# Attention by pairs of heads: probabilities copied out once as plain float32, value products with 64 output rows into the two halves of a bank, no fold by DMA

## The chip, the cores and the metric

The kernel runs on one core of one Trainium2 chip. The metric is the device time of one execution in microseconds: 4202.87 us in the median of three runs (4188.57 to 4209.19). Five engines work beside each other: PE (TensorE, matrix products and transposes into the eight banks of PSUM), DVE (VectorE), ACT (ScalarE), POOL (GpSimd), and SP, which issues the DMAs. Each runs its own instructions in order and waits at semaphores for the others.

## The reference

Two layers of a transformer-like trunk over 1152 tokens: 128 prompt tokens and 1024 sample tokens. A layer projects its input into three groups of heads, mixes each, projects back, and adds a feed-forward part. The three mixers are a gated recurrence (HGRN, 4 heads), attention with compressed keys and values (MLA, 6 heads, keys of 96 columns, values of 64) and attention with shared keys (GQA, 6 heads of 64 columns on 2 key heads). What the change touches is the attention, for both kinds:

```
s = jnp.einsum('bqhgd,bkhd->bhgqk', qi, k, preferred_element_type=F32) * scale
p = jax.nn.softmax(s, axis=-1)
return jnp.einsum('bhgqk,bkhe->bqhge', p.astype(v.dtype), v)
```

Sample queries (8 tiles of 128) read 128 cached keys and the 1024 sample keys, that is 9 key tiles; prompt queries (one tile) read the 128 prompt keys alone. All is float32.

## The kernel before

A layer has four phases: B (in-projection and HGRN), C (attention), D (output projection, first norm) and E (feed-forward, second norm). Large products are made in three terms of split operands: `split` rounds an operand to float32r (`hi`) and keeps the exact rest (`lo`), and `mm3` (L110 to L112) adds hi*hi, hi*lo and lo*hi. A float32r product is one pass on PE, a plain float32 product is recorded as two.

Phase C (`phase_c`) runs GQA, then MLA, through the same loop, `attention`. A *group* is one head and two query tiles; there are 24 groups in GQA and 24 in MLA in each layer. For a group, `probs` makes the scores of each query tile in three banks of 384 keys (L799; 2 products a bank in GQA, 3 in MLA), their maxima on DVE (L800, L803), and the exponentials with their sums on ACT (L805). The nine key tiles of the probabilities are then turned, two at a time, in five *turns* (`turn`): four transposes on PE into a bank `c` (L820), and the split of the bank into `hi` and `lo` (tiles `pt`). In four turns ACT rounds (L103) and DVE subtracts (L104). In the first turn of a group (`POOL_TURNS`) ACT copies the bank to `px` (L824), DVE rounds (L825) and Pool subtracts (L826). The value product (L869) has as its weights the 64 high and the 64 low columns of the values beside each other, so its 128 output rows are the products with the high and with the low part; it runs over the 256 columns of `hi` and again over those of `lo`. After nine key tiles DVE multiplies the bank `d` by the reciprocals of the sums (L873; `inv_sums` has brought them along the free axis through DRAM, `rind` and `rb`), a DMA moves one half of the rows across to the other partitions (L770), and Pool adds the halves (L771, `out_rows`) into the mixed activations `mx(j)`.

The scores run ahead of the turns by `LEAD` pieces (a piece is one bank of scores), the turns ahead of the value products by `AHEAD`; `NPT` and `NP` are the buffers of turned tiles and of probabilities. With every second turn one piece of other work (`self.aside`) is taken in: during GQA the backward states of HGRN (`hgrn_back`, L739 on PE), the turning of the second key head's queries and keys (`gqa_turn`), the turning of MLA's compressed operands (`mla_turn`) and the prompt's attention (`prompt_attention`: scores L884, transposes L899, values L906); during MLA each head's keys (`prep_k`), queries (`prep_q`, tiles `qg` of 512 columns and `qp` of the prompt), values (`prep_v`) and its prompt's attention. `prep_k` makes the keys of both heads of a pair, as the two halves of its output rows, and uses one half; it does so for each head.

The order of the instructions on each engine isn't that of the text: a scheduler places them within the limits of buffers and dependences. The PSUM banks of phase C are rings: scores in `b` (3) and `a` (2), turns in `c` (2), value sums in `d` (1).

Of the kernel before, what the change touches and what calls it, by code (L numbers as in the profile page):

```python
# [7 lines left out]
F32 = mybir.dt.float32  # L8
# [8 lines left out]
P = 128  # L17
D = 1024
# [20 lines left out]
W_OUT_ORDER = (0, 1, 7, 2, 5, 6, 3, 4)  # L39


def mixed(a, b, n):
    """n pieces of a, then one of b, and so on."""
# [10 lines left out]
class Build:  # L54
# [24 lines left out]
    def banks(self, **tags):  # L79
        """PSUM banks of the phase that starts: tag -> the rings its tiles come from, in turn."""  # L80
# [17 lines left out]
    def split(self, hi, lo, src, eng=None, vec=False):  # L98
        """hi = src rounded to float32r, lo = the exact rest."""
# [6 lines left out]
    def mm3(self, out, terms):  # L106
        """out = sum of a.T @ b over terms of split operands (ah, al, bh, bl)."""
# [6 lines left out]
    def rsq(self, out, ss, scale, cols):  # L114
        """out = (ss * scale + EPS) ** -0.5"""
# [37 lines left out]
    def floors(self):  # L153
        """the second layer's lower bounds of the gates, and one minus them."""
# [19 lines left out]
    def ada(self, l, part):  # L174
        """part: 0 sh1, 1 sc1, 2 g1, 3 sh2, 4 sc2, 5 g2. A generator of eight pieces of work."""
# [32 lines left out]
    def ada0(self):  # L208
        """the first layer's sh1 and sc1."""
# [44 lines left out]
    def coefs(self, l, which, ln):  # L254
        """(scale, shift) [P, 8, 2] of the modulation; with ln = (layer, norm) that norm's gain and bias are in them."""
# [12 lines left out]
    def make_hT(self, coefs, ci, xt, dst, phase):  # L268
        """dst [P, 8, 2, 384]: (x * scale + shift).T of the token tiles 3 ci .. 3 ci + 2."""
# [22 lines left out]
    def stats(self, u):  # L292
        """one over the deviation, and the mean, of the rows."""
# [10 lines left out]
    def norm(self, u):  # L304
        """layer norm without gain and bias, in place."""
# [17 lines left out]
    # ================= in-projection and HGRN =================  # L323
# [1118 lines left out]
```

## Time and profile before

| | |
|---|---|
| median of three runs | 4202.87 us (4188.57 to 4209.19) |
| span of the profiled execution | 4234.5 us |
| PE busy in it | 3772.9 us (89%) |
| DVE busy | 2251.7 us (53%) |
| ACT busy | 1587.9 us (38%) |
| POOL busy | 1330.6 us (31%) |

The busy time of an engine is the union of its instructions' records. PE's products overlap each other, and their ends are modelled, so a busy PE isn't a PE at its peak; how soon one product starts after the one before says more. Shares over the whole span mix phases with different limits, so the phases are read apart.

### The profile page before, as it was taken

The page shows a single profiled execution, that of the slowest core. Times are in us where ns is not written, and L with a number is a line of the kernel's source. Part 1 is how long each engine was busy: PE and PEld are TensorE (multiplying, and loading weights), DVE is VectorE, ACT ScalarE, POOL GpSimd, SP SyncE. Part 2 cuts the span into 40 slices and gives each one's busy share as a digit, 9 for nine tenths or more (in the row PEclk, how much of TensorE's full clock was granted, in tenths as well). Part 3 has the DMA queues.
Part 4 walks back from the last instruction along what each step waited for, and adds up shares of the span by engine and source line. Part 5 has one row for each costly group of instructions (what it writes and reads, how often), then busy time and mean ns, then how long its engine had stood idle before and what let it go on. Part 6 is the DMA issues. An engine that isn't in the chain of part 4 may idle for free. (4 is left out here: it accounts for less than half of the span.)

```text
span 4234.5 us, 58490 instructions
## 1 busy us (share of the span) xinstructions
PE 3772.9 (89%) x21820; PEld 3429.4 (81%) x21820; DVE 2251.7 (53%) x4256; ACT 1587.9 (37%) x3576; POOL 1330.6 (31%) x1558
## 2 busy tenths in 40 slices
PE   8999867777799999999999987777777999999997
PEld 7987756677679899999989877666766799999996
DVE  5688355555566434443366883654544743333336
ACT  5543455555433122122144335655553421111111
POOL 1277552232126000000432876513222650000043
PEclk9988988988899999999999988888888999999999
DMA  6322533211224222222331114221112221111121
GB/s 213 111 74 63 142 43 41 25 15 14 42 69 137 73 75 80 65 75 72 104 123 57 52 45 106 48 37 21 14 20 59 74 93 50 40 45 45 40 90 70
DMA packets 235207, 282.13 MB, mean 67 GB/s; under 512 B 98057, under 2 KB 163721, under 8 KB 234538
## 3 DMA queue, kind: packets, MB, share of 16 engines
q1 hardware_dynamic: 234922, 278.38, 24.9%
q8 instruction: 172, 2.82, 0.3%
q14 instruction: 113, 0.93, 0.1%
HBM read 231.05 MB, written 38.87 MB: 64 GB/s over the span
## 5 line engine op out<-in xcount | busy, mean ns | idle before, releaser
L111 PE MATMUL b<-h,w 128*128 128x384 f32 x1848 | 623.5, 337 | 5.2 <-DVE h L104 5.2
L112 PE MATMUL b<-h,w 128*128 128x384 f32 x1848 | 623.2, 337 | 2.1 <-DVE w L104 2.1
L110 PE MATMUL b<-h,w 128*128 128x384 f32 x1848 | 624.1, 338 | 0.4 <-ACT w L103 0.4
L104 DVE TENSOR_TENSOR w<-raw,w 128x1024 fp32r<-128x1024 f32 (+2 forms) x268 | 342.1, 1285 | 397.6 <-ACT w L103 337.6
L103 ACT CAST w<-raw 128x1024 fp32r<-128x1024 f32 (+2 forms) x272 | 281.4, 1039 | 675.7 <-PE b L111 236.2
L1258 POOL TENSOR_TENSOR acc<-acc,lg 128x512 f32<-128x512 f32 x36 | 50.8, 1428 | 1283.7 <-DVE acc L1244 1278.9
L111 PEld LDWEIGHTS b<-h,w 128*128 128x128 f32 x1848 | 348.5, 189 | 11.5 <-DVE h L104 6.4
L110 PEld LDWEIGHTS b<-h,w 128*128 128x128 f32 x1848 | 348.3, 189 | 9.9 <-issue 2.6
L112 PEld LDWEIGHTS b<-h,w 128*128 128x128 f32 x1848 | 348.5, 189 | 6.0 <-DVE w L104 2.4
L820 PE MATMUL c<-ident,p 128*128 128x128 f32 x1728 | 308.2, 302 | 35.6 <-ACT px L824 16.2
L104 DVE TENSOR_TENSOR pt<-c,pt 128x512 fp32r<-128x512 f32 (+2 forms) x404 | 240.4, 603 | 155.4 <-ACT pt L103 150.8
L110 PE MATMUL a<-w,h 128*128 128x256 f32 (+1 forms) x960 | 285.2, 297 | 2.9 <-ACT st L406 1.1
L103 ACT CAST pt<-c 128x512 fp32r<-128x512 f32 (+2 forms) x404 | 206.8, 526 | 211.3 <-PE c L820 180.2
L820 PEld LDWEIGHTS c<-ident,p 128*128 128x128 f32 x1728 | 231.5, 156 | 63.3 <-ACT px L824 19.8
L111 PE MATMUL a<-w,h 128*128 128x256 f32 (+1 forms) x960 | 282.6, 294 | 0.0
L112 PE MATMUL a<-w,h 128*128 128x256 f32 (+1 forms) x960 | 281.9, 294 | 0.0
L771 POOL TENSOR_TENSOR m<-u 64x256 f32<-64x256 f32 (+1 forms) x120 | 80.3, 669 | 621.0 <-DMA u<-u 555.1
L869 PE MATMUL d<-pt,V 128*128 128x256 f32 x864 | 202.0, 342 | 72.1 <-POOL pt L826 44.3
L800 DVE TENSOR_REDUCE m<-b 128x1 f32<-128x384 f32 x356 | 195.0, 553 | 117.2 <-PE b L799 114.9
L869 PE MATMUL d<-pt,v 128*128 128x256 f32 x864 | 188.7, 330 | 62.5 <-DVE u L873 21.6
L805 ACT ACTIVATE p<-b,nm 128x384 f32<-128x384 f32 x356 | 205.2, 585 | 98.5 <-DVE nm L803 77.5
L869 PEld LDWEIGHTS d<-pt,V 128*128 128x128 f32 x864 | 147.2, 221 | 87.1 <-POOL pt L826 49.9
(395 smaller groups left out, 9451.7 us busy)
## 6 DMA issues: line engine op xcount, KB each, us to landing
raw<-in_w_ffn_in_dram SPq DMA_DIRECT2D x88, 512.0 KB, 3.5
raw<-in_w_ada_dram SPq DMA_DIRECT2D x80, 512.0 KB, 3.8
raw<-in_w_ffn_out_dram SPq DMA_DIRECT2D x44, 512.0 KB, 4.7
raw<-in_w_in_a_dram SPq DMA_DIRECT2D x32, 512.0 KB, 3.9
rb<-rind SPq DMA_DIRECT2D x96, 128.0 KB, 5.1
xs<-acc SPq DMA_DIRECT2D x36, 256.0 KB, 4.1
u<-xs SPq DMA_DIRECT2D x36, 256.0 KB, 3.1
w<-in_w_ada_dram SPq DMA_DIRECT2D x16, 512.0 KB, 6.7
```

What stands on the lines that cost most here:

```text
L103: self.nc.scalar.copy(hi, src)
L104: (eng or self.nc.vector).tensor_tensor(lo, src, hi.bitcast(F32), op=ALU.subtract)
L110: self.nc.tensor.matmul(out, ah, bh, start=i == 0, stop=False)
L111: self.nc.tensor.matmul(out, ah, bl, start=False, stop=False)
L112: self.nc.tensor.matmul(out, al, bh, start=False, stop=i == n - 1)
L771: nc.gpsimd.tensor_tensor(self.mx(hd // 2)[r:r + 64, cols], On[r:r + 64], sw[r:r + 64], op=ALU.add)
L800: nc.vector.reduce_max(mx[:, c:c + 1], ps, axis=AX.X)
L805: nc.scalar.activation(pt[:, c * 384:(c + 1) * 384], tiles[c], AF.Exp, bias=nm, accum_out=sm[:, i, c:c + 1])
L820: nc.tensor.transpose(pt[:, (2 * a + i) * P:(2 * a + i + 1) * P], g["p"][i][:, kt * P:(kt + 1) * P], self.ident)
L869: nc.tensor.matmul(po[:, :256], g["v"](kt), w[:, i, a * 256:(a + 1) * 256], start=kt == 0 and i == 0, stop=kt == 8 and i == 1)
L1258: nc.gpsimd.tensor_tensor(acc[t][:, hs], acc[t][:, hs], g[:, min(t, 1)], op=ALU.mult)
```

## The change

A group becomes a pair of heads and one query tile. There are as many groups as before (24 and 24 a layer), as many scores and as many transposes. What differs:

- A turn takes two successive key tiles of the two heads, across the border of groups too, so 9 key tiles of a group make four and a half turns. The bank is copied out once, as plain float32, by ACT and DVE in turn.
- The value product is plain float32: weights 128 x 64 (one head's values, neither split nor doubled), 128 columns, and 64 output rows; the pair's even head goes to the lower half of a bank's partitions, the odd one to the upper half.
- The output is copied from the bank by DVE as it is; half a group later Pool multiplies it by the reciprocals, straight into `mx(j)`. The DMA across partitions and the addition are gone.
- MLA's keys are made once for a pair (four tiles `kE`, `kF` instead of two), its queries by 256 columns at the start of the group that first needs them. The prompt's attention is done for pairs.
- During GQA, the turning of the other key head's operands comes first, and `hgrn_back` after it.
- `AHEAD` counts turns of the new kind, and is 1 instead of 2; `LEAD`, `NPT` and `NP` are one smaller each. The places of the mixed activations, and with them the order of the rows of the output weights, are permuted.

```
-MX_SLOT = {0: 1, 1: 4, 2: 5, 3: 2, 4: 3, 5: 0}
+MX_SLOT = {0: 1, 1: 4, 2: 5, 3: 0, 4: 3, 5: 2}
-POOL_TURNS = (0,)
-AHEAD, LEAD, NPT, NP = 2, 7, 4, 6
+AHEAD, LEAD, NPT, NP = 1, 6, 3, 5
-W_OUT_ORDER = (0, 1, 7, 2, 5, 6, 3, 4)
+W_OUT_ORDER = (0, 1, 5, 2, 7, 6, 3, 4)
...
-    def out_rows(self, hd, cols, On, sw):
...
-    def inv_sums(self, sums, n):
+    def inv_sums(self, sums):
...
-        rb = self.t("att", [P, 256], tag="rb", bufs=2)
-        nc.sync.dma_start(rb[:, :n * P], d[:n].rearrange("a p -> (a p)").unsqueeze(0).broadcast_to([P, n * P]))
+        rb = self.t("att", [P, P], tag="rb", bufs=3)
+        for h in range(2):
+            nc.sync.dma_start(rb[h * 64:(h + 1) * 64], d[h:h + 1].broadcast_to([64, P]))
...
-    def turn(self, g, st):
+    def turn(self, n, steps):
         nc = self.nc
-        kts = [kt for kt in (2 * st, 2 * st + 1) if kt < 9]
-        n = len(kts) * 256
         pt = self.ps("T")
-        for a, kt in enumerate(kts):
-            for i in range(2):
-                nc.tensor.transpose(pt[:, (2 * a + i) * P:(2 * a + i + 1) * P], g["p"][i][:, kt * P:(kt + 1) * P], self.ident)
-        w = self.t("att", [P, 2, 512], F32R, tag="pt", bufs=NPT)
-        if st in POOL_TURNS:
-            x = self.t("att", [P, 512], tag="px", bufs=1)
-            nc.scalar.copy(x[:, :n], pt[:, :n])
-            nc.vector.tensor_copy(w[:, 0, :n], x[:, :n])
-            nc.gpsimd.tensor_tensor(w[:, 1, :n], x[:, :n], w[:, 0, :n].bitcast(F32), op=ALU.subtract)
+        for i, (g, kt) in enumerate(steps):
+            for u in range(2):
+                nc.tensor.transpose(pt[:, (2 * i + u) * P:(2 * i + u + 1) * P], g["p"][u][:, kt * P:(kt + 1) * P], self.ident)
+        w = self.t("att", [P, 512], tag="pt", bufs=NPT)
+        if n % 2:
+            nc.scalar.copy(w, pt)
         else:
-            self.split(w[:, 0, :n], w[:, 1, :n], pt[:, :n])
-        return kts, w
+            nc.vector.tensor_copy(w, pt)
+        return w
...
-            kts, w = turned[s]
-            turned[s] = None
-            for a, kt in enumerate(kts):
-                for i in range(2):
-                    nc.tensor.matmul(po[:, :256], g["v"](kt), w[:, i, a * 256:(a + 1) * 256],
-                                     start=kt == 0 and i == 0, stop=kt == 8 and i == 1)
-            if k == 4:
-                On = self.tmp("u")
-                nc.vector.tensor_tensor(On[:, :256], po[:, :256], g["rb"], op=ALU.mult)
-                self.out_rows(g["hd"], slice(g["q0"] * P, g["q0"] * P + 256), On[:, :256], On[:, 256:])
+            w = turned[s // 2]
+            for h in range(2):
+                o = (2 * (s % 2) + h) * P
+                nc.tensor.matmul(po[h * 64:(h + 1) * 64, :P], g["v"](k, h), w[:, o:o + P], start=k == 0, stop=k == 8)
+            if k == 4 and late:
+                late()
+                late = None
+            if k == 8:
+                On = self.t("att", [P, P], tag="On", bufs=2)
+                nc.vector.tensor_copy(On, po[:, :P])
+                def late(g=g, On=On):
+                    nc.gpsimd.tensor_tensor(self.mx(g["j"])[:, g["qt"] * P:(g["qt"] + 1) * P], On, g["rb"], op=ALU.mult)
...
-        def prep_k(hd, c, n):
-            e, pr = hd % 2, hd // 2
-            r = slice(e * 64, e * 64 + 64)
+        def prep_k(pr, c, n):
             w = [ukv[a][:, pr * P:(pr + 1) * P] for a in range(2)]
...
-            nc.scalar.copy(x[r, :n], ps[r, :n])
-            self.split(kf[r, 0, c:c + n], kf[r, 1, c:c + n], x[r, :n], eng=nc.gpsimd)
+            nc.scalar.copy(x[:, :n], ps[:, :n])
+            for e in range(2):
+                r = slice(e * 64, e * 64 + 64)
+                kf = kE[pr % 2][e].rearrange("p a t s -> p a (t s)")
+                self.split(kf[r, 0, c:c + n], kf[r, 1, c:c + n], x[r, :n], eng=nc.gpsimd)
...
+        def queries(pr, t0):
+            for i in range(2):
+                prep_q(2 * pr + i, t0, 256, "qg", 4)
...
-        for hd in range(6):
-            for q0 in (1, 3, 5, 7):
-                groups.append(dict(hd=hd, q0=q0, passes=mla_passes(hd), v=lambda kt, hd=hd: vt[hd][:, 1 + kt]))
-            groups[-4]["start"] = lambda hd=hd: start(hd)
-            groups[-3]["start"] = lambda hd=hd: prep_q(hd, 5, 512, "qg", 2)
+        for pr in range(3):
+            for qt in range(1, NT):
+                groups.append(dict(j=pr, qt=qt, passes=[mla_passes(2 * pr + i) for i in range(2)],
+                                   v=lambda kt, i, pr=pr: vt[pr][:, 1 + kt, i * 64:i * 64 + 64]))
+            groups[-8]["start"] = lambda pr=pr: start(pr)
+            for t0 in (3, 5, 7):
+                groups[t0 - 9]["start"] = lambda pr=pr, t0=t0: queries(pr, t0)
```

The order of instructions on PE shows what the value products become. In GQA of the first layer, before, with `p` the probabilities, `c` the bank of a turn, `pt` a turned tile, `V` the values and `d` the bank of the sums:

```order
L820 MATMUL c_7424<-ident_75,p_7271 128x128
L820 MATMUL c_7424<-ident_75,p_7350 128x128
L820 MATMUL c_7424<-ident_75,p_7271 128x128
L820 MATMUL c_7424<-ident_75,p_7350 128x128
L869 MATMUL d_7365<-pt_7379,V_5785 128x256 x3
L869 MATMUL d_7365<-pt_7413,V_5785 128x256
L820 MATMUL c_7473<-ident_75,p_7271 128x128
```

and at the like place of the changed kernel, where the transposes are L812, the scores L793 and the value products L859:

```order
L793 MATMUL b_7225<-K_1234_5787,Q_5786 128x384
L793 MATMUL b_7225<-K_1235_5788,Q_5786 128x384
L859 MATMUL d_7131<-pt_7165,V_5785 64x128 x4
L812 MATMUL c_7212<-ident_75,p_7109 128x128
L812 MATMUL c_7212<-ident_75,p_7153 128x128
L812 MATMUL c_7212<-ident_75,p_7109 128x128
L812 MATMUL c_7212<-ident_75,p_7153 128x128
L793 MATMUL b_7241<-K_1234_5787,Q_5786 128x384
L793 MATMUL b_7241<-K_1235_5788,Q_5786 128x384
L859 MATMUL d_7131<-pt_7198,V_5785 64x128 x4
```

Before, each value product writes all 128 rows of a bank, and the run of a turned tile is cut by transposes. Afterwards four products of 64 rows stand together, two key tiles for each half of the bank, between products that fill 128 rows. Over the whole program there are 403 such runs, counted by where the number of output rows changes between 64 and 128.

On DVE, at the end of a group before (`u` the scaled sums, `rb` the reciprocals):

```order
L104 TENSOR_TENSOR pt_7075<-c_7070,pt_7075 128x512
L104 TENSOR_TENSOR pt_7092<-c_7087,pt_7092 128x512
L800 TENSOR_REDUCE m_1669_7351<-a_7370 128x1
L104 TENSOR_TENSOR pt_7141<-c_7138,pt_7141 128x256
L800 TENSOR_REDUCE m_1669_7351<-b_7386 128x1
L873 TENSOR_TENSOR u_7199<-d_7078,rb_6983 128x256
L825 CAST pt_7157<-px_7158 128x512
```

and after (`On` the sums as copied):

```order
L794 TENSOR_REDUCE m_1618_7154<-a_7172 128x1
L797 TENSOR_REDUCE nm_7111<-m_1606_7110 128x1
L865 COPY On_7129<-d_7033 128x128
L817 COPY pt_7147<-c_7142 128x512
L794 TENSOR_REDUCE m_1618_7154<-a_7176 128x1
L797 TENSOR_REDUCE nm_7155<-m_1618_7154 128x1
L817 COPY pt_7198<-c_7193 128x512
```

Every turn's subtraction is replaced by a copy for every second turn, and the instruction that empties `d` reads no reciprocals any more.

More of the change, by code (lines that the diff above doesn't have):

```diff
@@ L847, in advance @@
                 done += 1
-        steps = [(gi, k) for gi in range(len(groups)) for k in range(5)]
+        steps = [(gi, k) for gi in range(len(groups)) for k in range(9)]
         turned = []
         def turn_to(n):
-            while len(turned) < min(n, len(steps)):
-                gi, k = steps[len(turned)]
-                advance(6 * gi + LEAD + (6 * (k + 1)) // 5)
-                turned.append(self.turn(groups[gi], k))
+            while len(turned) < min(n, len(steps) // 2):
+                two = steps[2 * len(turned):2 * len(turned) + 2]
+                gi, k = two[1]
+                advance(6 * gi + LEAD + (6 * (k + 1)) // 9)
+                turned.append(self.turn(len(turned), [(groups[gi], k) for gi, k in two]))
+        late = None
         for s, (gi, k) in enumerate(steps):
             g = groups[gi]
-            turn_to(s + 1 + AHEAD)
-            if s % 2:
+            if s % 2 == 0:
+                turn_to(s // 2 + 1 + AHEAD)
                 next(self.aside, None)
@@ L984, in gqa_passes, with prompts, passes, aside1 @@
             return f
-        def prompts(g):
-            Q, K = self.gqa[g]
-            for hs in ((0, 1), (2,)):
-                yield from self.prompt_attention(
-                    [6 + 3 * g + i for i in hs],
-                    lambda i, hs=hs: [(Q[:, hs[i], 0:P], K[k][:, 0]) for k in range(2)],
-                    lambda i: V[:, g, 0].rearrange("p a f -> p (a f)"))
-        def turns():
-            yield from self.hgrn_back(l)
+        def prompts(p):
+            def passes(i):
+                hd = 2 * p + i
+                Q, K = self.gqa[hd // 3]
+                return [(Q[:, hd % 3, 0:P], K[k][:, 0]) for k in range(2)]
+            yield from self.prompt_attention(3 + p, passes, lambda i: V[:, 0, (2 * p + i) // 3 * 64:(2 * p + i) // 3 * 64 + 64])
+        def aside1():
             for slot in range(10):
@@ L998, in turns @@
                 yield
-        def aside1():
-            yield from mixed(turns(), prompts(1), 3)
+            yield "turned"
+            yield from mixed(self.hgrn_back(l), chain(prompts(2), prompts(1)), 2)
         def aside0():
@@ L1008, in second, with third @@
         def second():
+            while next(self.aside, "turned") != "turned":
+                pass
+        def third():
             for _ in self.aside:
@@ L1013, in phase_c @@
         groups = []
-        for hd in (3, 4, 5, 0, 1, 2):
-            for q0 in (1, 3, 5, 7):
-                groups.append(dict(hd=6 + hd, q0=q0, passes=gqa_passes(hd),
-                                   v=lambda kt, g=hd // 3: V[:, g, 1 + kt].rearrange("p a f -> p (a f)")))
+        for p in (2, 1, 0):
+            for qt in range(1, NT):
+                groups.append(dict(j=3 + p, qt=qt, passes=[gqa_passes(2 * p + i) for i in range(2)],
+                                   v=lambda kt, i, p=p: V[:, 1 + kt, (2 * p + i) // 3 * 64:(2 * p + i) // 3 * 64 + 64]))
         groups[0]["values"] = values
-        groups[12]["start"] = second
+        groups[8]["start"] = second
+        groups[16]["start"] = third
         self.aside = aside1()
@@ L1052, in prep_v @@
                 self.mm3(ps[:, i * P:(i + 1) * P], [(cT[:, 0, s0 + i], cT[:, 1, s0 + i], ukv[0][:, sl], ukv[1][:, sl])])
[L1053 to L1058 removed]
+            nc.scalar.copy(vt[pr][:, s0:s0 + n], ps[:, :n * P].rearrange("p (t c) -> p t c", c=P))
         def prep_q(hd, t0, n, tag, bufs):
@@ L1078, in mla_passes @@
         def mla_passes(hd):
-            e = hd % 2
-            kf = [kE[e].rearrange("p a t s -> p a (t s)")[:, a] for a in range(2)]
+            kf = [kE[hd // 2 % 2][hd % 2].rearrange("p a t s -> p a (t s)")[:, a] for a in range(2)]
             def f(qt):
-                t0 = 1 if qt < 5 else 5
+                t0 = qt - (qt + 1) % 2
                 q = qt_[(hd, t0)]
@@ L1115, in start @@
                 pass
-            self.aside = prep(hd + 1) if hd < 5 else iter(())
+            queries(pr, 1)
+            self.aside = prep(pr + 1) if pr < 2 else iter(())
+        def queries(pr, t0):
+            for i in range(2):
+                prep_q(2 * pr + i, t0, 256, "qg", 4)
         def values():
```

125 lines of the change are left out of this document (51 added, 74 removed).

## The prediction

> **What bounds the kernel now.** The change touches only the two attention phases, so the first view is the summary by 40 slices: it shows where they lie.
>
> ```profile
> PE   8999867777799999999999987777777999999997
> PEclk9988988988899999999999988888888999999999
> ```
>
> TensorE is nine tenths busy or more almost everywhere, except in slices 5 to 12 and 25 to 31. By the source lines these hold the attention phases; the first score product (L799) and the last value product (L869) of each layer set the two windows of the next view.
>
> ```profile
> core 0: us, PE busy (x) PEld busy (x) DVE busy (x) ACT busy (x) POOL busy (x), PEclk, DMA share, GB/s
> 459.00:1159.00 700.00, 516.61 (x3084) 463.10 (x3082) 361.57 (x876) 378.40 (x1055) 237.11 (x327) 0.85 0.27 40
> 2570.00:3252.00 682.00, 502.21 (x2957) 451.90 (x2956) 355.29 (x866) 370.72 (x1032) 226.59 (x304) 0.85 0.23 35
> sum 1382.00, PE 1018.82 PEld 915.00 DVE 716.86 ACT 749.12 POOL 463.70; mean PE 509.41 PEld 457.50 DVE 358.43 ACT 374.56 POOL 231.85
> ```
>
> 1382 us lie in these phases. PE is busy for 74% of them, ACT for 54%, DVE for 52%: nothing is full, and PE's own clock is granted at 0.85 only. PE's busy time also counts the tail of each product, so its real stream is shorter still. The phase is therefore a chain: PE issues in order, and stands where an operand isn't there. The groups of instructions say for whom it stands (the last numbers: idle us just before, and who ended it).
>
> ```profile
> L869 PE MATMUL d<-pt,V 128*128 128x256 f32 x864 | 202.0, 342 | 72.1 <-POOL pt L826 44.3 <-ACT pt L103 21.2 <-DVE u L873 2.7
> L869 PE MATMUL d<-pt,v 128*128 128x256 f32 x864 | 188.7, 330 | 62.5 <-DVE u L873 21.6 <-POOL pt L826 20.5 <-DVE pt L825 19.5
> L820 PE MATMUL c<-ident,p 128*128 128x128 f32 x1728 | 308.2, 302 | 35.6 <-ACT px L824 16.2 <-DVE pt L104 8.0 <-ACT p L805 5.0
> L884 PE MATMUL b<-kE,qp 128*128 128x128 f32 x24 | 6.5, 328 | 25.2 <-POOL qp L104 12.9 <-ACT qp L103 12.3
> L884 PE MATMUL a<-kE,qp 128*128 128x128 f32 x12 | 2.8, 287 | 15.2 <-POOL qp L104 15.2
> L899 PE MATMUL c<-ident,t 128*128 128x128 f32 x24 | 7.7, 351 | 22.8 <-POOL t L895 21.7 <-ACT px L824 0.9
> L739 PE MATMUL c<-Sb,m 128*128 128x128 f32 x64 | 12.8, 332 | 29.8 <-POOL Sb L745 27.9 <-DVE pt L104 1.2 <-DVE nm L803 0.4
> ```
>
> The value products (L869) stand for 134.6 us, most of it for the splitting of the turned probabilities; the prompt's small attention (L884, L899) for 63.2 us. The HGRN chain (L739) remains.
>
> **The change, part by part: the work off PE.**
>
> ```profile
> L824 ACT COPY px<-c 128x512 f32<-128x512 f32 x96 | 56.8, 592 | 24.4 <-PE c L820 24.0
> L825 DVE CAST pt<-px 128x512 fp32r<-128x512 f32 x96 | 49.4, 514 | 14.5 <-ACT px L824 13.9
> L826 POOL TENSOR_TENSOR pt<-px,pt 128x512 fp32r<-128x512 f32 x96 | 123.7, 1288 | 147.9 <-DVE pt L825 127.0 <-DVE nm L803 20.1
> L103 ACT CAST pt<-c 128x512 fp32r<-128x512 f32 x288 | 166.4, 593 | 157.1 <-PE c L820 156.1
> L104 DVE TENSOR_TENSOR pt<-c,pt 128x512 fp32r<-128x512 f32 x288 | 194.3, 684 | 82.9 <-ACT pt L103 81.3 <-issue 0.3
> L873 DVE TENSOR_TENSOR u<-d,rb 128x256 f32<-128x256 f32 x96 | 40.4, 420 | 96.7 <-DMA rb<-rind 67.7 <-PE d L869 14.4 <-issue 13.0
> L1234 DVE COPY acc<-c 128x512 f32<-128x512 f32 x20 | 13.8, 690 | 16.7 <-PE c L112 16.6
> L908 DVE COPY u<-b 128x128 f32<-128x128 f32 x8 | 2.3, 284 | 2.2 <-PE b L906 2.2
> ```
>
> Now a turned tile of 512 columns takes two engines in a row, 0.593 + 0.684 = 1.28 us, or on the Pool way three, 0.592 + 0.514 + 1.288 = 2.39 us, before the last value product may go. Afterwards it takes one copy: 0.592 on ACT or 0.690 on DVE (the row of L1234, same shape from PSUM). A turn's lead shrinks from two turns to one, but its latency halves or better. 432 turns then cost ACT 216 x 0.592 = 128 us, where the four casts and copies above took 166.4 + 56.8 and more for the narrow ones; DVE loses 194.3 + 49.4 and gets 216 x 0.690 = 149. The end of a group waits no longer for the reciprocals' DMA: L873, which stood 67.7 us for it, becomes a 0.28 us copy (L908's shape), and Pool multiplies later. One wait is added, Pool's multiplication for the reciprocals:
>
> ```profile
> rb<-rind SPq DMA_DIRECT2D x96, 128.0 KB, 5.1
> ```
>
> They land 5.1 us after their issue, which follows the group's last exponential, while the multiplication is issued half a group after the group's last value product; a group takes 1382 / 96 = 14.4 us. So it stands there in time. Were it late, Pool's low halves of keys and queries queue behind it, and the scores for them: the L739 row bounds that by 29.8 us.
>
> All this is off PE; it counts only through PE's waits:
>
> - Gone are the waits for L826 (44.3 + 20.5), for L825 (19.5) and for L873 (2.7 + 21.6): 108.6 us.
> - The waits for ACT's cast (21.2) and of the transposes for the copies out of their bank (16.2 + 8.0) keep a cause, one copy instead of two. I take half: 22.7 us.
> - The prompt's attention comes for pairs: three chains a layer in MLA instead of six. Half of 25.2 + 15.2 + 22.8 is 31.6 us.
>
> Together 163 us of waits. What is late next is PE itself.
>
> **On PE.** Two places of the trace price the new value products: the one plain-float32 product that uses few columns of the array (L193, two passes of 512 columns), and HGRN's products on half of the array's rows (L652).
>
> ```profile
> L193 PE MATMUL d<-t,fold 4*2 4x512 f32 x16 | 8.1, 586 | 1.3 <-DVE t L188 1.3
> ```
>
> and the order of time on PE at both places (start, us, what):
>
> ```profile
> 104.00 0.28 PE L112 MATMUL a<-w,h 128*128 128x256 f32 x1
> 104.12 0.28 PE L110 MATMUL a<-w,h 128*128 128x256 f32 x1
> 104.33 1.02 PE L193 MATMUL d<-t,fold 4*2 4x512 f32 x2
> 105.27 0.39 PE L111 MATMUL a<-w,h 128*128 128x256 f32 x1
> 105.50 0.28 PE L112 MATMUL a<-w,h 128*128 128x256 f32 x1
> ...
> 382.44 0.28 PE L111 MATMUL a<-w,h 128*128 128x256 f32 x1
> 383.05 0.72 PE L652 MATMUL b<-Q,X 64*128 64x128 f32 x8 [0.33 <-POOL X L645]
> 383.70 0.39 PE L112 MATMUL a<-w,h 128*128 128x256 f32 x1
> 383.92 0.28 PE L110 MATMUL a<-w,h 128*128 128x256 f32 x1
> ```
>
> A float32r product of 256 columns follows the one before by 0.12 us. Plain float32 takes two passes; L193's two last 1.02 us together, one alone 0.586 with its tail, so a pass streams in 0.43 us, 0.84 ns a column: 0.107 us for 128 columns. Eight such passes in a row would need 0.86 us and a tail; L652's eight, four on each half of the rows, end after 0.72, tail included. Halves of the array work side by side.
>
> *Streaming.* Before: 1728 products x 0.12 = 207 us. After: a pair of key tiles has four passes in each column half; side by side 4 x 0.107 = 0.43 us, 432 times: 186 us. That is -22. In a row it would be 372, +165.
>
> *Changes of the array's division.* Transposes and scores use the whole array, the new value products half its columns, and in the built order these stand in 403 separate runs. One run costs, by L193: on the way in 104.33 - 104.12 - 0.12 = 0.09; on the way out (its second pass starts 0.43 after the first, at 104.76) 105.27 - 104.76 - 0.43 = 0.08, and 0.11 more for the weights loaded in the open (105.50 - 105.27 - 0.12). That is 0.28. The run's own first load is short there (2 columns); L652's first pass, with 128 columns, shows some 0.10 of it, 64 columns perhaps half. So 0.28 to 0.38, taken 0.33: 133 us. Where PE waits for the copy anyway, the way in (0.14) costs nothing; I take that for half of the runs, -28. Leaves +105.
>
> The row says 0.28 at least for a run. The Trainium skill, "TensorEngine Tiling (Array Packing)", section "Key Properties", says that changing the tiling mode, and not just the tile, drains the engine, which speaks against this change; by the drain of about 128 cycles that "TensorE: Matmul & The Clock Gate" gives in its Part 2, two drains would be an estimated 0.107 us a run, and this term 43 us instead of 105. The row contains the exposed loads too, and decides.
>
> *MLA's keys* are made once for a pair: per layer three passes over 1280 key columns fall away.
>
> ```profile
> 1500.22 0.34 PE L110 MATMUL b<-h,w 128*128 128x384 f32 x1
> 1500.39 0.34 PE L111 MATMUL b<-h,w 128*128 128x384 f32 x1
> ```
>
> 384 columns go in 0.17, so 1280 in three products take 3 x 0.58 = 1.7 us; x 3 x 2 layers = -10. The queries are made by 256 columns rather than 512, as many columns in all, but at the start of the very group that needs them (`queries`); before, those of tiles 5 to 8 came a group ahead and those of tiles 1 to 4 a head ahead. 24 times a group's first scores now stand behind this chain, whose end in tiles of 512 columns is:
>
> ```profile
> L103 ACT CAST qg<-t 128x512 fp32r<-128x512 f32 x24 | 14.9, 622 | 3.4 <-PE a L799 1.8 <-PE b L799 1.3 <-ACT t L1054 0.3
> L104 POOL TENSOR_TENSOR qg<-t,qg 128x512 fp32r<-128x512 f32 x24 | 31.7, 1319 | 22.2 <-ACT qg L103 17.8 <-issue 4.2
> ```
>
> Two more evacuations like L873's (0.42 for 256 columns) stand ahead; half of 0.622 and 1.319 makes 2 x 0.42 + 0.97 = 1.8 us. Behind the first scores on PE stand transposes and value products of the group before, which are ready and are partly ordered ahead; they hide it, or else it costs 24 x 1.8 = 43 us. I take a third, +15. SP issues three DMAs a group as before (a second half of the reciprocals for the fold), and the moved HGRN and key turning lie beside other work: nothing, bounded by L739's 29.8 us either way.
>
> **Sum:** PE -22 + 105 - 10 + 15 = +88; waits -163; together **-75 us**. The profiled execution's span is 4234.5 us, 32 us above the median of the runs shown (4202.87); no view says where these lie, so the difference goes onto the median: **4128 us**. About 0.5% (21 us) is what a measurement of this kernel can tell from no change.
>
> **The rivals.**
>
> *The column halves run one after the other (slower).* Place: L869's successor. L652 shows halves of the rows, no row shows halves of the columns. Price: 432 x (0.86 - 0.43) = +186, so 4128 + 186 = 4314. It decides from 0.60 us for two key tiles on (0.43 + 75 / 432). Against it stands L652's eight passes in 0.72 us. 18%. The Trainium skill, "TensorE: Matmul & The Clock Gate", Part 3, gives 2.38 times for three column tiles, an estimate of 0.54 us for two key tiles here and 4175 us for the whole; no run here shows it.
>
> *The waits move (no change).* PE, sooner at the value products, stands for scores or exponentials instead: the lead is one turn, scores run one piece less ahead, five tiles of probabilities instead of six. If only half of the 163 us goes, -82 + 88 = +6: 4209; if none, 4291. For it: neither ACT nor DVE was full, so the loop had other waits. Against it: ACT and DVE lose work, so exponentials and maxima come sooner. 20%.
>
> *More than the sum (faster).* With fewer stops PE's clock rises from 0.85; 0.05 more of it on 1018.8 us of PE time is 51 us, and the other half of the copies' waits 23: 4128 - 74 = 4054. 20%.
>
> The forecast itself has 42%, at 4078 to 4178 (L739's 30 us and the price of a run, 403 x 0.05 = 20, either way). The range takes in the fast rival with some more, and reaches up to the moved waits, but leaves most of the halves in a row out: 3990 to 4290. Faster by over 0.5%: forecast 0.41, fast rival 0.20, some of the moved waits 0.02, 0.63. Slower: 0.18 and 0.06 of the moved waits, 0.24. Within: 0.13.
>
> **What would show it.** Value products 64 x 128 whose two halves start within some 0.02 us of each other, and four key-tile passes in 0.43 us, prove the streaming; starts 0.107 apart over all eight refute it. After a run of them a 0.2 us step to the next whole-array product proves the price. No wait of PE for Pool or for reciprocals at value products; if their idle time instead stands at L793 (scores) or L812 (transposes) on exponentials, the waits moved. A wrong prediction would come from the price of a run (0.19 more each is 75 us) or from waits that I count as gone.

## The result, and the profile after

The changed kernel takes 4085.1 us (4082.26 to 4092.84, 4 runs), the kernel before 4195.72 us on the same chip (4178.04 to 4209.19, 4 runs): a ratio of 0.9736, with a 95% interval of 0.9704 to 0.9768, or 111 us less. Predicted were 4128 us, and 3990 to 4290. The spans of the two profiled executions are 4080.5 and 4234.5 us, 154 apart.

The attention phases of the changed kernel by windows (us, then the busy time and number of instructions of PE, of its weight loads PEld, of DVE, ACT and POOL, the granted clock, the DMA share, GB/s):

```profile
458.70:1086.60 627.90, 511.44 (x3989) 410.15 (x3989) 299.47 (x740) 313.92 (x907) 144.12 (x257) 0.90 0.20 36
2490.70:3089.80 599.10, 490.10 (x3865) 391.16 (x3865) 292.95 (x730) 305.25 (x885) 134.74 (x233) 0.90 0.19 31
sum 1227.00, PE 1001.55 PEld 801.31 DVE 592.42 ACT 619.17 POOL 278.85; mean PE 500.77 PEld 400.65 DVE 296.21 ACT 309.59 POOL 139.43
```

1382 us of attention became 1227, which is the whole difference: outside it the spans are 4234.5 - 1382 = 2852.5 and 4080.5 - 1227 = 2853.5. The granted clock rose from 0.85 to 0.90. Each phase splits once more, at the first score product that reads MLA's keys, into GQA and MLA. PE by windows, before first (GQA, MLA, GQA, MLA), after below:

```profile
459.30:810.80 351.50, 253.72 (x1512) 0.85 0.36 57
810.80:1158.90 348.10, 262.49 (x1572) 0.86 0.18 22
2569.90:2890.50 320.60, 235.39 (x1388) 0.86 0.31 50
2890.50:3251.90 361.40, 266.82 (x1573) 0.84 0.16 22
```

```profile
458.70:805.30 346.60, 255.02 (x1950) 0.86 0.25 52
805.30:1086.60 281.30, 256.43 (x2040) 0.94 0.13 16
2490.70:2814.10 323.40, 234.99 (x1826) 0.86 0.23 43
2814.10:3089.80 275.70, 255.12 (x2040) 0.95 0.14 16
```

The GQA stretches stayed as wholes (351.5 + 320.6 = 672 before, 670 after). The MLA stretches became shorter: 709.5 to 557.0. A view of the whole phase hides that half of it gained nothing on balance. The groups of instructions after (the last numbers again idle us and who ended it):

```profile
L859 PE MATMUL d<-pt,V 128*64 128x128 f32 x1728 | 152.9, 303 | 23.2 <-DMA V<-zk 15.4 <-DVE pt L817 4.4 <-DVE nm L797 1.5
L859 PE MATMUL d<-pt,v 128*64 128x128 f32 x1728 | 141.2, 289 | 10.6 <-ACT pt L815 8.7 <-DVE pt L817 1.3
L812 PE MATMUL c<-ident,p 128*128 128x128 f32 x1728 | 297.1, 293 | 9.3 <-ACT p L799 6.0 <-DVE pt L817 2.4 <-ACT pt L815 0.4
L878 PE MATMUL b<-kE,qp 128*128 128x128 f32 x12 | 2.0, 277 | 0.5 <-POOL qp L103 0.5
L893 PE MATMUL c<-ident,t 128*128 128x128 f32 x24 | 6.4, 310 | 0.3 <-ACT pt L815 0.2
L793 PE MATMUL b<-kE,qg 128*128 128x384 f32 x348 | 92.1, 382 | 45.0 <-ACT qg L102 33.7 <-POOL qg L103 7.2 <-ACT p L799 4.1
L922 PE MATMUL c<-ident,t 128*128 128x128 f32 x36 | 7.3, 335 | 42.8 <-DMA t<-zm 42.8
L868 POOL TENSOR_TENSOR m<-On,rb 128x128 f32<-128x128 f32 x96 | 43.9, 457 | 740.0 <-DMA rb<-rind 375.3 <-DVE On L865 199.0 <-DVE m L794 39.6
```

The waits at value products went from 134.6 to 33.8, at transposes from 35.6 to 9.3, at the prompt's products from 63.2 to 0.8. New or longer are waits for queries (L793, 45.0) and for loads of MLA's compressed operands (L922, 42.8). The two longest waits for queries, 16.75 and 16.52 us, end at MLA's first scores in the two layers, where the stretches are split, so they count to GQA. And Pool stands 375 us for reciprocals.

### The profile page after: what moved, and what is told of

Its sections match the earlier page's. It is cut to its first block, busy times and chain, and to the rows that moved or that the text cites. A ratio compares the mean times of both kernels' runs of the same rounds, so it can differ in the third digit from the quotient of the medians.

```text
span 4080.5 us, 61021 instructions
## 1 busy us (share of the span) xinstructions
PE 3751.3 (92%) x23638; PEld 3310.7 (81%) x23638; DVE 2125.7 (52%) x3984; ACT 1457.5 (36%) x3278; POOL 1144.9 (28%) x1418
## 4 chain that ended last, share of the span: by engine, by line
PE 63%; DMA 11%; DVE 7%; POOL 4%; ACT 3%; issue 2%; SPq 1%; POOLq 0%; DVEq 0%; ACTq 0%
PE b L109 9%; PE b L111 9%; PE b L110 9%; DMA rind<-rin 7%; PE a L109 3%; PE a L111 3%; PE a L110 3%; PE c L812 3%; PE d L859 3%; PE b L793 3%; PE c L109 2%; PE c L111 2%; PE c L110 2%; PE a L793 2%; PE d L110 2%
## 5 line engine op out<-in xcount | busy, mean ns | idle before, releaser
L812 PE MATMUL c<-ident,p 128*128 128x128 f32 x1728 | 297.1, 293 | 9.3 <-ACT p L799 6.0
L812 PEld LDWEIGHTS c<-ident,p 128*128 128x128 f32 x1728 | 203.1, 147 | 68.8 <-issue 44.8
L868 POOL TENSOR_TENSOR m<-On,rb 128x128 f32<-128x128 f32 x96 | 43.9, 457 | 740.0 <-DMA rb<-rind 375.3
L794 DVE TENSOR_REDUCE m<-b 128x1 f32<-128x384 f32 x346 | 185.9, 552 | 115.6 <-PE b L793 113.7
L817 DVE COPY pt<-c 128x512 f32<-128x512 f32 x216 | 148.6, 688 | 106.1 <-PE c L812 84.3
L109 PEld LDWEIGHTS a<-w,h 128*128 128x128 f32 x960 | 188.3, 196 | 11.3 <-issue 3.0
L110 PEld LDWEIGHTS a<-w,h 128*128 128x128 f32 x960 | 188.0, 196 | 6.6 <-issue 1.9
L111 PEld LDWEIGHTS a<-w,h 128*128 128x128 f32 x960 | 187.4, 195 | 4.0 <-issue 0.2
L815 ACT COPY pt<-c 128x512 f32<-128x512 f32 x216 | 126.9, 587 | 174.8 <-PE c L812 132.8
```

The lines of the kernel that those rows point to most:

```text
L109: self.nc.tensor.matmul(out, ah, bh, start=i == 0, stop=False)
L110: self.nc.tensor.matmul(out, ah, bl, start=False, stop=False)
L111: self.nc.tensor.matmul(out, al, bh, start=False, stop=i == n - 1)
L794: nc.vector.reduce_max(mx[:, c:c + 1], ps, axis=AX.X)
L812: nc.tensor.transpose(pt[:, (2 * i + u) * P:(2 * i + u + 1) * P], g["p"][u][:, kt * P:(kt + 1) * P], self.ident)
L815: nc.scalar.copy(w, pt)
```

## The experiments

Medians are in us; the ratio is to the kernel before in the same series, since chips differ by some tens of us. The runs of the repeat of before, e1, e2 and e3 are one series; e4 to e7 and e8 to e10 are two more, and e11 the last.

| run | edit | median | before | ratio | 95% interval |
|---|---|---|---|---|---|
| e1 | before, no turns by way of Pool | 4125.12 | 4153.55 | 0.9928 | 0.9907 to 0.9949 |
| e2 | after, copy by two engines in a row | 4055.24 | 4153.55 | 0.9763 | 0.9741 to 0.9784 |
| e3 | after, outputs scaled at once | 4147.82 | 4153.55 | 0.9972 | 0.9954 to 0.9990 |
| e4 | after | 4051.79 | 4150.80 | 0.9760 | 0.9729 to 0.9791 |
| e5 | e1, with outputs scaled late | 4111.46 | 4150.80 | 0.9897 | 0.9870 to 0.9925 |
| e6 | after, MLA's values on the whole array | 4051.83 | 4150.80 | 0.9746 | 0.9719 to 0.9772 |
| e7 | after, two turns' values together | 4047.96 | 4150.80 | 0.9745 | 0.9718 to 0.9772 |
| e8 | after, prompts head by head | 4060.53 | 4154.69 | 0.9772 | 0.9758 to 0.9787 |
| e9 | after, queries a group early | 4049.50 | 4154.69 | 0.9743 | 0.9727 to 0.9760 |
| e10 | after, side loads ahead | 4023.45 | 4154.69 | 0.9682 | 0.9667 to 0.9697 |
| e11 | before, without the fold's transfer | 4093.86 | 4181.59 | 0.9788 | 0.9765 to 0.9812 |

**The kernel before once more.**

> The kernel before, unchanged, to have a second profile of it beside the others. The recorded profiles differ by 154 us (4234.5 to 4080.5), the runs by 111 us (4195.7 to 4085.1). If the first profile of before was a slow sample, this one's span is near 4195 and its two attention windows together are near 1340 us instead of 1382; if the profile slows this kernel more than the changed one, it is near 4235 again.

4157.08 us, among 4145 to 4170 of its series, at a span of 4155.3. So the profile doesn't slow this kernel, and the second case falls. The 4234.5 of the first profile lie above all four runs of before in the first series (4178 to 4209), too; whether that is the chip or that one execution stays open. The same change is worth 111 us there and 99 on the chip of e4.

**e1: no way over Pool.**

```
-POOL_TURNS = (0,)
+POOL_TURNS = ()
```

> Before, with every turned tile split by ACT and DVE and none by the way over Pool. Theory A (the gain is that the turned tile is ready sooner): the 65 us of PE's waits for Pool and the 20 us for DVE's rounding go, ACT and DVE get work instead; 30 to 60 us faster than before. Rival B (the gain comes from pairs: prompts, keys, the order of the other work): within 15 us of before.

28 us less, between the two theories: three engines in a row cost something, but not most of it.

**e2: the copy takes two engines.** In the changed kernel:

```
-            nc.scalar.copy(w, pt)          (or vector.tensor_copy, in turn)
+        x = self.tmp("u")
+        nc.scalar.copy(x, pt)
+        nc.vector.tensor_copy(w, x)
```

> After, with the turned tile copied twice, by ACT out of the bank and then by DVE into the tile that the value products read; result unchanged. Theory A: the latency (0.59 + about 0.45 us) and the load on both engines come back, 60 to 110 us slower than the changed kernel, and PE's waits at the value products return. Rival B: at most 20 us slower.

0.9763 beside 0.9760 of e4: nothing. In the changed kernel the latency of the copy, on which the prediction had put the value products' waits, costs nothing that shows. What the waits of before came from, this run alone can't say.

**e3: scaled at the group's end.** In the changed kernel DVE multiplies straight from the bank, as before the change:

```
-                On = self.t("att", [P, P], tag="On", bufs=2)
-                nc.vector.tensor_copy(On, po[:, :P])
+                nc.vector.tensor_tensor(self.mx(g["j"])[...], po[:, :P], g["rb"], op=ALU.mult)
```

> After, with the output scaled by DVE straight out of the bank at the end of the group, so that the bank is freed only when the reciprocals have landed. Theory A: the 24 us of PE's waits behind that instruction come back, 15 to 30 us slower than the changed kernel. Rival: the reciprocals have landed long before with groups of one query tile, nothing or a few us faster, since Pool's multiplication and one copy are saved.

It gives back 0.9972 - 0.9760, some 88 us: far beyond the 15 to 30. By groups, DVE's multiplication, and by waits of PE (for whom, us in total, times, longest) what follows from it:

```profile
L864 DVE TENSOR_TENSOR m<-d,rb 128x128 f32<-128x128 f32 x96 | 27.8, 290 | 267.0 <-DMA rb<-rind 219.1 <-PE d L859 23.0 <-PE b L793 17.3
```

```profile
PE c L812 <- ACT p L799: 51.4, 16, 5.2
PE d L859 <- DVE m L864: 49.7, 26, 5.4
```

DVE works in order. While it stands 219 us for the reciprocals, the maxima behind it are late, then ACT's exponentials, then PE. In before the same instruction (L873) stood 67.7 us for them. So this price belongs to the new form; e5 asks what it was in the old one.

**e4: the changed kernel again.**

> The changed kernel itself, on the chip of this series, so that its variants stand beside it. Both theories expect the ratio of the first result, 0.9736 to within 0.004. With it the run with a copy on two engines (ratio 0.9763) can be placed: if a slower copy of the turned tile costs nearly nothing, as theory B says, this run comes within 20 us of that one; by theory A (the latency of the copy was what the old kernel paid for) it would be 60 us or more below it.

0.9760, within what was expected of it; theory A falls, as e2's 0.9763 is 0.0003 from it, 1 us. That the pairs are the gain, as theory B has it, isn't shown by this.

**e5: late scaling in before.** With no turns over Pool, outputs copied out at once, and multiplied and folded by Pool a step into the next group:

```
+            if k == 1 and late:
+                late()
+                late = None
             if k == 4:
-                On = self.tmp("u")
-                nc.vector.tensor_tensor(On[:, :256], po[:, :256], g["rb"], op=ALU.mult)
-                self.out_rows(...)
+                On = self.t("att", [P, 256], tag="On", bufs=2)
+                nc.vector.tensor_copy(On, po[:, :256])
+                def late(g=g, On=On):
+                    nc.gpsimd.tensor_tensor(On, On, g["rb"], op=ALU.mult)
+                    self.out_rows(...)
```

> The kernel before, with all turns on the ACT and DVE way (as in the run without the Pool way, 28 us faster than before), and with one part of the change put into it: a group's outputs are copied out of the bank by VectorE at once, and GpSimd multiplies them by the reciprocals and folds them one step into the next group. Theory R: VectorE, which works in order, stood at a group's end for the reciprocals' DMA (54 to 68 us of it in the two profiles of before), and held up the maxima and copies behind it. Then this kernel is 25 to 60 us faster than the one without the Pool way, 4065 to 4100 where before is 4153. Theory S: the waits of before came from the split of the turned tile over two engines, and the reciprocals only looked late. Then it is within 15 us of that one, 4110 to 4140.

0.9897 against 0.9928 of e1, about 13 us, with intervals that overlap: theory R falls for the kernel before. Its trace named the next suspect: Pool still stood 530 us for the fold's transfer.

**e6: MLA's value products on the whole array.**

```
+            if "whole" in g:
+                nc.tensor.matmul(po[:, :256], g["whole"](k), w[:, s % 2 * 256:s % 2 * 256 + 256], start=k == 0, stop=k == 8)
...
```

> The changed kernel, with the value products of the MLA half as one plain float32 product of 256 columns by all 128 value columns, in place of two of 128 columns into the halves of a bank; of the product the two quarters that count are copied out. In MLA the array is then not divided any more, and each of 216 turns takes 0.86 us of columns instead of 0.43. If a run of divided products costs the 0.30 us that the trace of after shows on its way in, out and in loads, this is 216 x (0.86 - 0.43 - 0.30) = 28 us slower than the changed kernel (15 to 45). If changing the division costs nearly nothing beside the streaming, it is 70 to 95 us slower. If PE has slack there and waits for others, it is within 10 us.

The same time as e4 to 0.1 us in the medians, though each of the 216 turns streams 0.43 us more, 93 us in all: the third case by its number. The windows of the two MLA stretches, in e4 and below in this run:

```profile
795.50:1072.30 276.80, 255.76 (x2040) 0.94 0.13 17
2787.20:3058.80 271.60, 251.62 (x2042) 0.96 0.14 17
```

```profile
792.20:1062.60 270.40, 261.27 (x1610) 0.99 0.12 17
2778.10:3052.70 274.60, 263.62 (x1610) 0.98 0.11 17
```

PE is busy 525 us of 545; in e4 it is busy 507 of 548. So the third case has its reason in part: PE stood 41 us in e4 and stands 20 here. That dividing the array is free doesn't fit all the same: of the 93 us only 18 show in the busy time, so 75 were saved, an estimated 75 / 216 = 0.35 a turn. The higher clock (0.99 and 0.98) has a share in that, an estimated 0.035 x 525 = 18 us, without which it is 0.26.

**e7: two turns' value products together.**

```
-            if s % 2 == 0:
-                turn_to(s // 2 + 1 + AHEAD)
-                next(self.aside, None)
+            if s % 4 == 0:
+                for a in (1, 2):
+                    turn_to(s // 2 + a + AHEAD)
+                    next(self.aside, None)
```

> The changed kernel, with the value products of two turns issued one after the other, after the transposes of the next two turns: half as many runs of divided products, some 200 instead of 403. If a run's price of 0.30 us is real and PE is the bound, this saves 200 x 0.19 to 0.30 = 38 to 60 us, less what the shorter lead of a turned tile (three buffers for four turns in hand) gives back: 20 to 50 us faster than the changed kernel. If the price of a run is hidden or the lead decides, it is 0 to 40 us slower.

Inconclusive: the scheduler took them apart again. In the trace PE changes to products of 64 rows 367 times, where the changed kernel does so 396 times. The 4 us less are within the noise of the two runs, and say nothing of 200.

**e8: prompts head by head.**

```
             for i in range(2):
                 prep_q(2 * pr + i, 0, P, "qp", 2)
-            qs = [qt_[(2 * pr + i, 0)] for i in range(2)]
-            yield from self.prompt_attention(pr, ...)
+                q = qt_[(2 * pr + i, 0)]
+                yield from self.prompt_attention(pr, ..., (i,))
...
```

> The changed kernel, with the prompt's part in MLA done head by head again (two chains of scores, exponentials, scaling, turn and product per pair, where the change does one). On one chip the profiles of before and after differ in the MLA stretches alone (670 us in before, 548 in after), while the GQA stretches are 634 and 645; and in before's MLA stretches the longest waits of TensorE are those for a prompt's queries and probabilities, each followed by a stretch at a halved clock. Theory P: these chains, one per head, were a main cost; then this kernel is 25 to 60 us slower than the changed kernel, 4077 to 4112 where that is 4052. Theory Q: they cost only because VectorE and GpSimd were crowded with the split and the reciprocals' wait, which this kernel leaves out; then it is at most 12 us slower.

9 us more than e4: theory Q, by its number. Halving the number of the prompt's chains is not what removed their waits. (The two profiles that the expectation compares, of e0 and e4, are of two chips, not of one; the medians of before are 3 us apart there.)

**e9: queries a group early.**

```
-                groups[t0 - 9]["start"] = lambda pr=pr, t0=t0: queries(pr, t0)
+                groups[t0 - 9 - (t0 > 3)]["start"] = lambda pr=pr, t0=t0: queries(pr, t0)
+            if pr < 2:
+                groups[-1]["start"] = lambda pr=pr: queries(pr + 1, 1)
...
```

> The changed kernel, with the queries of MLA's fifth and seventh query tiles, and the first of the next pair, made one group earlier than the change does (the third stays as it is). The prediction priced the queries just in time at 15 us, with a bound of 43; the profile of the changed kernel shows 45 us of waits for them, of which two of some 15 us stand ahead of MLA's first scores and can't be helped by this. If the rest counts, and a halved clock behind each with it, this is 8 to 25 us faster than the changed kernel; if other work only moves into those places, it is within 8.

2 us less than e4 in the medians, 0.0017 in the ratio: within the 8 of the second expectation. The two longest waits for queries in after, those ahead of MLA's first scores, can't be helped by this.

**e10: side loads ahead.**

```
+        xs = [jobs[0][0](*jobs[0][2])]
+        for n, (_, use, a) in enumerate(jobs):
+            if n + 1 < len(jobs):
+                xs.append(jobs[n + 1][0](*jobs[n + 1][2]))
+            use(*a, xs[n])
+            yield
```

(`jobs` holds the old loads and transposes of `mla_turn` as pairs of functions.)

> The changed kernel, with the loads of the piece of work that turns MLA's compressed queries and keys issued one piece ahead. In the GQA stretches of the changed kernel TensorE waits 43 us for these loads, 13 and 9 for others of its kind (before: 16 for the same), and the granted clock is 0.87 there. If fewer and shorter GQA steps leave the side work less cover, as I think now, this kernel is 15 to 50 us faster than the changed one. If the loads are late because the queue of transfers is full, and not because they are issued late, it is within 10.

28 us less than e4, a ratio of 0.9682: faster than both kernels. By the profiles 18 of them lie in the GQA stretches (645 in e4, 627 here). The loads also take their buffers from another ring (`u`), which may have a part in it. Their wait falls but doesn't go; the waits of PE:

```profile
PE c L927 <- DMA u<-zm: 26.8, 3, 16.0
PE c L955 <- DMA u<-zk: 13.9, 8, 3.7
```

**e11: before, without the fold's transfer.** Pool adds the first half to itself; the output lacks the low half of the values.

```
-        o = 64 - r
-        nc.sync.dma_start(sw[r:r + 64], On[o:o + 64])
-        nc.gpsimd.tensor_tensor(self.mx(hd // 2)[r:r + 64, cols], On[r:r + 64], sw[r:r + 64], op=ALU.add)
+        nc.gpsimd.tensor_tensor(self.mx(hd // 2)[r:r + 64, cols], On[r:r + 64], On[r:r + 64], op=ALU.add)
```

> The kernel before, with one thing left out: the transfer that brings a group's second half to the rows of the first. GpSimd adds the first half to itself instead, so that its instructions and their durations stay; the output lacks the low half of the values. In the first profile of before GpSimd stands 555 us for this transfer, and it works in order: the keys, queries and prompt probabilities that it splits or scales for MLA stand behind it. Theory F: this is the main part of what the change gained and the other runs did not find; then this kernel is 40 to 90 us faster than before, 4065 to 4115 where before is 4154, nearly all of it in the MLA stretches, where the waits for split queries and scaled prompt probabilities go. Theory L: the gain is the sum of lighter work on all three engines, and GpSimd's standing is idle time that nobody waits for; then it is within 15 us of before.

88 us less than before, theory F. Windows of its GQA, MLA, GQA, MLA stretches (PE):

```profile
463.60:795.70 332.10, 253.21 (x1512) 0.87 0.35 55
795.70:1094.30 298.60, 247.45 (x1573) 0.91 0.19 20
2496.40:2798.00 301.60, 231.31 (x1388) 0.87 0.30 47
2798.00:3099.70 301.70, 251.81 (x1572) 0.89 0.20 21
```

MLA takes 600 us, GQA 634; the repeat of before (on another chip, where before takes 28 us less) had 670 (334.4 + 336.0) and 634 (328.9 + 304.8). The changed kernel's MLA takes 548 (e4), so 52 us of MLA's gain are not in this run. Waits of PE in this run:

```profile
PE d L867 <- DVE u L871: 40.4, 14, 9.8
PE c L897 <- POOL t L893: 14.5, 7, 4.6
PE d L867 <- POOL pt L824: 5.2, 8, 1.0
PE b L882 <- ACT qp L103: 4.8, 4, 1.7
```

The wait for Pool's low halves is 5.2 us (in before L826: 44.3 + 20.5, in its repeat 36.0 + 9.2), though Pool still makes them. The edit also takes one issue a group out of the queue of SP. The prompt's waits shrink likewise. What took their place is DVE's scaling (L871): with the swap gone, the reciprocals are next, and the change takes that away too.

## Why the prediction was right, step by step

**Right by its steps:** only the attention phases change; the halves run side by side; a run has a price; value products wait little. The order of time on PE after:

```profile
867.15 0.34 PE L793 MATMUL b<-kE,qg 128*128 128x384 f32 x1
867.42 0.66 PE L859 MATMUL d<-pt,v 128*64 128x128 f32 x8
...
867.80 0.28 PE L859 MATMUL d<-pt,v 128*64 128x128 f32 x2
868.01 0.88 PE L812 MATMUL c<-ident,p 128*128 128x128 f32 x6
```

The last two of the eight passes start within 0.01 us of each other, 0.38 after the first two: three steps of 0.11 and 0.05 of weights loaded in the open. That is the predicted 0.43 for two key tiles, and no halves in a row. The way in is 867.42 - 867.15 - 0.17 = 0.10, the way out 868.01 - 867.80 - 0.11 = 0.10. With the 0.05 these are 0.25. The load behind the way out comes on top, which these grouped rows don't show: the second transpose starts 0.17 after the first instead of 0.11 (median of 171 such places in this trace), 0.06 more. That makes 0.31, where 0.33 was taken, and e6's estimates lie at 0.26 and 0.35. "TensorEngine Tiling (Array Packing)", "Key Properties", in the Trainium skill, has the drain but no price; the 128 cycles of "TensorE: Matmul & The Clock Gate", Part 2, an estimated 0.053 a change, are half of what the rows show.

**Right in sum, in part by luck, and wrong in cause: the waits.** 163 us were to go; of the three kinds together (134.6 + 35.6 + 63.2 = 233) 190 went. But the step "Gone are the waits for L826", which took them for the Pool way's three engines, mistook their cause, and so did the prompt's half for "three chains a layer in MLA instead of six". e1, e2 and e8 give 28, 1 and 9 us for these. e11 gives 88 for a transfer that the prediction had no term for. Both were to be read from before. Waits of Pool there:

```profile
POOL m L771 <- DMA u<-u: 555.1, 86, 17.1
```

and one such place, by time on each engine (start, us, what, idle us and who ended it; SPq is SP's issuing of DMAs):

```profile
847.39 0.36 SPq L779 DMA_DIRECT2D rind<-rin  x1
850.31 0.42 DVE L873 TENSOR_TENSOR u<-d,rb 128x256 f32<-128x256 f32 x1
855.52 0.33 SPq L781 DMA_DIRECT2D rb<-rind  x1
855.95 2.16 SPq L770 DMA_DIRECT2D u<-u  x1
861.18 0.71 POOL L771 TENSOR_TENSOR m<-u 64x256 f32<-64x256 f32 x1 [7.59 <-DMA u<-u]
861.97 0.72 POOL L104 TENSOR_TENSOR kE<-t,kE 64x256 fp32r<-64x256 f32 x1
862.72 0.34 DVE L1071 TENSOR_SCALAR t<-b,still 64x128 f32<-64x128 f32 x1 [6.74 <-POOL kE L104]
863.10 0.27 ACT L1075 ACTIVATE t<-b 64x128 f32<-64x128 f32 x1 [4.99 <-DVE t L1071]
863.75 0.69 PE L884 MATMUL b<-kE,qp 128*128 128x128 f32 x2 [6.63 <-ACT qp L103]
```

Pool stands for the fold's transfer. The keys' split behind it, which needs nothing of it, is late; DVE can't have the buffer `t` until then, ACT follows DVE, and PE waits 6.6 us "for ACT". The last releaser was innocent. The prediction names this queue on Pool ("low halves of keys and queries queue behind it"), but only for the new multiplication, bounded there by a row of HGRN (L739) that has no part in it, and not for the fold that stood there already. What queues is in the main MLA's work (keys, queries, prompts by Pool), which fits that MLA gained. In GQA, too, the value products' wait for L826 (44.3 us) is gone; what took its place there stands below.

The fold's transfer is itself held up. The sums were ready at 850.31 + 0.42 = 850.73, but SP, in order, stood for `rind` to land and only then issued `rb`, at 855.52, and the fold's transfer behind it, at 855.95: 5.2 of the 10.45 us until Pool's addition are SP's standing. So it is at 29 of the 96 folds (5.2 us in the median). No run moves the transfer ahead in that queue, so how much of the 88 us this would have brought isn't shown.

**The clock was in the rival only.** The 6.6 us aren't the whole price. The same place by windows (PE) and by time:

```profile
852.00:856.00 4.00, 3.77 (x28) 1.00 0.05 2
860.00:864.00 4.00, 0.25 (x1) 0.50 0.04 12
868.00:872.00 4.00, 3.88 (x12) 0.50 0.00 0
876.00:880.00 4.00, 4.00 (x28) 1.00 0.12 31
```

```profile
864.99 0.63 PE L110 MATMUL b<-ckvT,w 128*128 128x512 f32 x1
865.41 0.63 PE L111 MATMUL b<-ckvT,w 128*128 128x512 f32 x1
...
875.33 0.40 PE L111 MATMUL a<-ckvT,w 128*128 128x512 f32 x1
875.57 0.40 PE L112 MATMUL a<-ckvT,w 128*128 128x512 f32 x1
```

After the stop PE goes at half its clock until past 872: 512 columns take 0.42 us there and 0.24 later. "TensorE: Matmul & The Clock Gate", Part 1, in the Trainium skill has a rule for this: half rate after a window of some 3.4 us without work, full rate after a busy one. The trace agrees with the window: 81 of the 82 stretches at half clock in before last a whole number of 3.41 us. It doesn't agree that a whole window must be without work: here the half clock began at 859.07, 1.9 us after the last product's end at 857.13, and it ended at 872.73, 9 us after the products had come back. (1 - 0.85) x 1382 = 207 us of clock were withheld in before's phases, 0.10 x 1227 = 123 after, part of it while PE stood anyway. The prediction gave the clock only to the rival "more than the sum"; it belongs with every wait of several us.

**Wrong: "So it stands there in time".** Only the second of two transfers was counted. The issues of DMAs in before (us from issue to landing last):

```profile
rind<-rin SPq DMA_DIRECT2D x96, 1.0 KB, 9.3
rb<-rind SPq DMA_DIRECT2D x96, 128.0 KB, 5.1
```

9.3 + 5.1 = 14.4 us is a whole group (8.3 + 3.7 in e4), and Pool stands 375 us after the change. That PE hardly notices (7.7 us for Pool at queries and prompts, L793 and L878) I put down to the place; no run tests that on Pool. In the trace of after, the multiplication starts 0.4 us ahead of the products of the next group's fifth key tile (median over the groups, by the starts of L868 and L859), and Pool has no turns to serve any more. In before, a fold started 9.0 us behind its group's last value product (median, by the starts of L771 and L869), so what stood behind it on Pool came at least as late. With the multiplication on DVE the same lateness costs 88 us (e3).

**Too small: what the side work costs.** Queries were put at +15; the waits show 45.0 (L793), of which 33 stand ahead of MLA's first scores, where before had no wait; making the others earlier brings 2 (e9). The moved work beside GQA was put at "nothing": the wait for loads at L922 went from 15.8 (L932) to 42.8, that for the loads of `gqa_turn` from 3.3 to 23.6, and one of 15.4 for the loads of `V` is new. Loading ahead for the first of these brings 28 us (e10). Together 33 + 27 + 20 + 15 = 95 us of new waits lie in the GQA stretches, against some 64 that went from its value products and 16 from HGRN's chain (L739, 27.9 to 11.7 for Pool). With the price of the runs that fits a GQA that gained nothing; e10 shows it by a run for the loads alone.

So the forecast's 75 came out as 111 (99 on the chip of e4). More waits went than were counted (190 against 163), and less clock was withheld, against side work that cost more. How the 111 divide between these isn't shown. Nor are the 88 of e11 a share of the 99: putting the multiplication back on DVE at once gives back 88 as well (e3), with no fold there at all. So in the new form late scaling is needed for most of the gain, though it was worth 13 us in the old one (e5). The parts overlap, late scaling, the Pool way, the fold and the prices on PE, and no run puts the fold into the changed form and leaves the rest.

## What to carry to other kernels

A wait is named by who came last, not by who was late: follow it back over the in-order engines, and look for one that stands for a DMA round trip with unrelated work behind it. Look at the queue that issues the DMAs, too: it is in order like the others. Such a step goes to a place, or an engine, where nothing behind it is due. Count for each stop of PE of several us the time at half clock behind it, and split a phase by its parts before pricing, since the loss may lie in one of them.

## What was not expected of the hardware

- A 1.0 KB transfer that turns 2 x 128 values into rows takes 9.3 us to land, longer than the 128 KB one behind it (5.1).
- Column halves of the array start within 0.01 us of each other, but changing to them and back costs 0.10 us each way, and loads in the open besides, 0.31 in all for a run; in MLA the divided products and whole ones of twice the streaming take the same time (e6).
- Keeping the whole array in use raised MLA's granted clock from 0.94 and 0.96 to 0.99 and 0.98 at the same time. Whether it is the fuller array or only fewer stops, no run tells.
